# Hybrid decoder block on one core: pacing the streamed w_ada, and the order of the first projection stage

## The chip, the cores and the metric

The kernel runs on one core of a Trainium2 chip. The metric is the device time of one execution in microseconds (us). The core has a matrix engine (TensorE, in the profile PE, with its weight loads apart as PEld), VectorE (DVE), ScalarE (ACT), GpSimd (POOL) and SyncE (SP); here SP issues nearly all DMA transfers. PE accumulates in PSUM, which has eight banks.

## The reference, cut to what matters

One decoder layer for 256 tokens of width 2048, in float32. A conditioning vector c gives six modulation vectors; two projections of the normed x feed an attention and a retention branch, which are gated, merged and projected; a gated MLP with a causal convolution follows.

```python
mod = silu(c) @ w_ada + b_ada                       # 2048 x 12288
shift1, scale1, gate1, shift2, scale2, gate2 = split(mod, 6)
h = rms_norm(x, norm1_g) * (1 + scale1) + shift1
qa, ka, va, qr, kr, vr, gr, ga_logit, gb_logit = split(h @ w_in)
ya = attention(norm(qa), norm(ka), va) @ w_attn_br
yr = (group_norm(retention(rot(qr), rot(kr), vr)) * silu(gr)) @ w_ret_br
x = x + gate1 * ((sigmoid(ga_logit) * ya + sigmoid(gb_logit) * yr) @ w_o)
h2 = rms_norm(x, norm2_g) * (1 + scale2) + shift2
val, gt = split(causal_conv(h2 @ w_up))
x = x + gate2 * ((silu(gt) * val) @ w_down)
```

## The kernel before, in words

Every weight comes from memory once, in chunks of 128 partitions x 1024 columns (512 KB), through a pool of nine buffers (`raw`) that SP refills in order: a transfer is issued when the buffer of the ninth transfer before it is free. A weight chunk is split into two float32r parts, `hi` by a cast on ScalarE and `lo` by a subtraction on VectorE (`split`, lines 142 to 145; four buffers each), and PE runs three products per chunk: hi x h_h, hi x h_l, lo x h_h. The raw buffer is free when VectorE has made `lo`.

**w_ada is not multiplied on PE.** Its rows stand as 96 tiles of 128 outputs, two halves of 1024 each (`ada`, lines 192 to 201). A half is loaded into a `raw` buffer and VectorE multiplies it with silu(c) and sums along the row, in one pass. These passes are a paced generator in the class `Side` (lines 51 to 89): every weight chunk calls `side.pump()`, which adds the rate to what is due (line 82) and draws a pass for each whole unit (lines 83 to 85). `side.until` (lines 66 to 70) draws without pace until a condition holds. Three rates exist: `ADA_FIRST` for the tiles of shift1 and scale1 (64 halves), `ADA_RATE` from va on for gate1, shift2, scale2 and gate2 (128 halves, `rest_of_mod`, line 498), `ADA_LAST` behind the second norm. gate1 is asked for ahead of o_0 (line 712), and all up to scale2 ahead of o_3 (line 729): 96 of the 128.

**The first projection stage** (lines 479 to 493) makes 6144 columns for queries, keys, retention's queries and keys, and gr: six groups (g) of two blocks of 512 columns, for two halves of the tokens (t), so that a group takes four PSUM banks. The depth of 2048 is 16 tiles (k), and h's tiles appear one by one as w_ada's passes end (`modulated`, `norm_tile`). So the stage goes in three steps over k, `STEPS` (line 29): tiles 0 to 3, 4 to 9 and 10 to 15; in each step all six groups. In step 0 groups 0 and 1 share their chunks in turn, and then the others follow one by one. The first two tiles (`PLAIN`) run in plain float32 from the unsplit chunk. At a group's end `g_out` (line 469) brings the four banks into `acc`: by a copy on ScalarE in step 0, by a sum on VectorE later. `turn_x` (lines 309 to 324) scales and transposes x, a quarter of its columns at a time; quarters 0 and 1 come ahead of the stage, 2 and 3 ahead of groups 2 and 3 of step 0. At the end of a group in the last step `beside_groups` starts the side work on it (norms, turns, rotation), which also advances by `side.pump()`.

What stands between: va, attention, vr, retention, ya and ga, yr and gb; then the output projection o_0 to o_3 (line 725 on), the second norm in an order written out by hand (lines 787 to 836), and the MLP (up, dn).

The order on each engine is set by a scheduler from priorities, except for instructions marked `keep_in_program_order`, which stand in the order of the code on their engine; w_ada's passes are so marked, and chained.

Of the kernel before, what the change touches and what calls it, by code (L numbers as in the profile page):

```python
# [11 lines left out]
F32 = mybir.dt.float32  # L12
F32R = mybir.dt.float32r
AF = mybir.ActivationFunctionType
ALU = mybir.AluOpType
AX = mybir.AxisListType

P = 128
D = 2048
S = 256  # L20
KC = D // P
# [4 lines left out]
EPS = 1e-6  # L26
NG = 6
NB = 512
STEPS = ((0, 4), (4, 10), (10, 16))
PLAIN = 2  # L30
ADA_FIRST = 0.8
ADA_RATE = 0.46
ADA_LAST = 0.38
SIDE_AHEAD = 150
SKEW = 4
# [57 lines left out]
def block_kernel(ctx, tc, a, out):  # L93
    nc = tc.nc
# [9 lines left out]
    def unit(name, dt=F32, shape=(P, 2, S)):  # L104
        return upool.tile(list(shape), dt, tag="u", name=name)

    def tmp(name, shape=(P, S), dt=F32):
        return tpool.tile(list(shape), dt, tag="t", name=name)
# [4 lines left out]
    def bank(name):  # L113
        return psum.tile([P, 512], F32, tag="ps", name=name)
# [10 lines left out]
    ident = cpool.tile([P, P], F32, name="ident")  # L125
# [12 lines left out]
    def seq(ins):  # L138

        return tc.keep_in_program_order(ins) if ordered[0] else ins  # L140

    def split(hi, lo, src):

        return (seq(nc.scalar.copy(hi, src)),  # L144
                seq(nc.vector.tensor_tensor(lo, src, hi.bitcast(F32), op=ALU.subtract)))  # L145
# [39 lines left out]
    def chain(ins):  # L185

        if behind[0] is not None:
            tc.add_manual_dep(ins.ins, behind[0].ins.name, mybir.DependencyInfo(
                mybir.DependencyClass.NoSync, mybir.DependencyReason.DATA), reason="w_ada in order")
        behind[0] = ins  # L190
# [92 lines left out]
    def norm_tile(k):  # L283
        m = mod6[:, 0:2, k]
        chain(nc.vector.tensor_tensor(m, parts6[:, 0:2, k, 0], parts6[:, 0:2, k, 1], op=ALU.add))
        chain(nc.vector.tensor_tensor(m, m, bada6[:, 0:2, k], op=ALU.add))
        scale = mod6[:, 1, k:k + 1]
        chain(nc.vector.tensor_tensor(scale, scale, sm[:, C_G1 + k:C_G1 + k + 1], op=ALU.mult))
        t = plain[:, k] if k < PLAIN else tmp(f"ht_{k}")
        nc.scalar.activation(t, turned[k // 2][:, k % 2 * S:(k % 2 + 1) * S], AF.Identity,  # L290
                             bias=mod6[:, 0, k:k + 1], scale=mod6[:, 1, k:k + 1])
        h = unit(f"h1_{k}", F32R)
        split(h[:, 0], h[:, 1], t)
        return h[:, 0], h[:, 1]

    def modulated():
# [9 lines left out]
    nc.vector.tensor_reduce(rstd, ssq0.rearrange("p (t n) -> p t n", n=4), axis=AX.X, op=ALU.add)  # L306
    rstd_of(rstd, rstd, 1.0 / D)

    def turn_x(q):

        xs = []
        for t in range(2):
            xs.append(tmp(f"xn1_{q}_{t}", (P, NB)))
            ins = nc.scalar.activation(xs[t], x2[:, t, q * NB:(q + 1) * NB], AF.Copy, scale=rstd[:, t:t + 1])
            if q > 1:
                tc.keep_in_program_order(ins)
        for i in range(2):
            pt = bank(f"xn_t{q}_{i}")
            for j in range(2):
                for t in range(2):  # L320
                    s = slice((2 * i + j) * P, (2 * i + j + 1) * P)
                    nc.tensor.transpose(pt[:, (2 * j + t) * P:(2 * j + t + 1) * P], xs[t][:, s], ident)
            turned.append(unit(f"xnT_{q}_{i}", shape=(P, NB)))
            nc.scalar.copy(turned[-1], pt)

    for q in range(2):
        turn_x(q)

    acc = [[None, None] for _ in range(12)]

# [24 lines left out]
    def query_heads(n):  # L355
        for t in range(2):
            sq = tmp(f"qksq_{n}_{t}", (P, NB))
            nc.scalar.activation(sq, acc[n][t], AF.Square)
            nc.vector.tensor_reduce(ssq1[:, t, 4 * n:4 * n + 4], sq.rearrange("p (h d) -> p h d", d=P), axis=AX.X,
                                    op=ALU.add)  # L360
        yield 1
        if n < 2:
            qT[2 * n:2 * n + 2] = heads_of(n, "q")
            yield 1

    def key_scales():
        rstd_of(ssq1.rearrange("p t h -> p (t h)"), ssq1.rearrange("p t h -> p (t h)"), 1.0 / P)
        nc.vector.scalar_tensor_tensor(gg, sm[:, C_GQ:C_GQ + 1], P ** -0.5, sm[:, C_GK:C_GK + 1],
                                       op0=ALU.mult, op1=ALU.mult)
        for n in range(2, 4):  # L370
            for t in range(2):
                k = acc[n][t].rearrange("p (h d) -> p h d", d=P)
                nc.vector.tensor_tensor(k, k, ssq1[:, t, 4 * n:4 * n + 4].unsqueeze(2).to_broadcast([P, 4, P]),
                                        op=ALU.mult)
        yield 3
        for n in range(2, 4):
            kT[2 * n - 4:2 * n - 2] = heads_of(n, "k", gg)
            yield 1
# [22 lines left out]
    def bias_rows():  # L401
        psr = bank("psr")
        nc.tensor.matmul(psr[:HEADS, :383], rel, onehot, start=True, stop=True)
        brow = tmp("brow", (HEADS, 383))
        nc.vector.tensor_tensor(brow, psr[:HEADS, :383], maskrow, op=ALU.add)
        nc.sync.dma_start(bdram, brow)
        yield 1
# [14 lines left out]
    def rotated(n):  # L422
        for t in range(2):
            x = acc[n][t]
            xs = x.rearrange("p (h s d) -> p h s d", s=2, d=P // 2)
            x8 = x.rearrange("p (a d) -> p a d", d=P // 2)
            sw = tmp(f"sw_{n}_{t}", (P, 4, 2, P // 2))
            sn = sinT[:, t].rearrange("p (s d) -> p s d", s=2)
            for s in range(2):
                nc.vector.tensor_tensor(sw[:, :, s], xs[:, :, 1 - s], sn[:, s].unsqueeze(1).to_broadcast([P, 4, P // 2]),  # L430
                                        op=ALU.mult)
            nc.vector.tensor_tensor(x8, x8, cosT[:, t].unsqueeze(1).to_broadcast([P, 8, P // 2]), op=ALU.mult)
            nc.vector.tensor_tensor(x8, x8, sw.rearrange("p h s d -> p (h s) d"), op=ALU.add)
            yield 2
# [6 lines left out]
    def beside_groups(g):  # L441
        if g < 2:
            side.add(query_heads(2 * g))
            side.add(query_heads(2 * g + 1))
        elif g < 4:
            if g == 2:
                side.add(bias_rows())
                side.add(key_scales())
            side.add(rotated(2 * g))
            side.add(rotated(2 * g + 1))  # L450

    def g_chunk(banks, g, k, first, last):
        side.until(lambda: len(h1) > k)
        if k < PLAIN:
            raw = load(a["w_g"][k, g], 1024, f"g_{g}_{k}")
            for t in range(2):
                for j in range(2):
                    nc.tensor.matmul(banks[j][t], plain[:, k, t * P:(t + 1) * P], raw[:, j * NB:(j + 1) * NB],  # L458
                                     start=first, stop=last)
        else:  # L460
            hi, lo = load_split(a["w_g"][k, g], 1024, f"g_{g}_{k}")
            for part, w in ((0, hi), (1, hi), (0, lo)):
                for t in range(2):
                    for j in range(2):
                        nc.tensor.matmul(banks[j][t], tok(h1[k], part, t), w[:, j * NB:(j + 1) * NB],  # L465
                                         start=(first and part == 0 and w is hi), stop=(last and w is lo))
        side.pump()

    def g_out(step, g, banks):
        for j in range(2):  # L470
            for t in range(2):
                n = 2 * g + j
                if step == 0:
                    acc[n][t] = unit(f"acc_{n}_{t}", shape=(P, NB))
                    nc.scalar.copy(acc[n][t], banks[j][t])
                else:
                    nc.vector.tensor_tensor(acc[n][t], banks[j][t], acc[n][t], op=ALU.add)

    for step, (ka, kb) in enumerate(STEPS):
        if step == 1:  # L480
            tables()

        for gs in ((0, 1), (2,), (3,), (4,), (5,)) if step == 0 else tuple((g,) for g in range(NG)):
            if step == 0 and gs[0] in (2, 3):
                turn_x(gs[0])
            banks = {g: [[bank(f"g{step}_{g}_{j}_{t}") for t in range(2)] for j in range(2)] for g in gs}
            for k in range(ka, kb):
                for g in gs:
                    g_chunk(banks[g], g, k, k == ka, k == kb - 1)
                    if k == kb - 1:  # L490
                        g_out(step, g, banks[g])
                        if kb == KC:
                            beside_groups(g)
    side.until(lambda: len(h1) == KC)

    mods = [2 * KC]
# [21 lines left out]
    side.drain()  # L518
    side.pace(rest_of_mod(), ADA_RATE)
    for n in range(4, 8):  # L520
# [465 lines left out]
```

## Time and profile before

| | us |
|---|---|
| median of 3 runs | 1657.1 (1656.17 to 1658.59) |
| the profiled execution's own time | 1653.88 |
| its span | 1652.1 |
| PE busy | 1600.3 (97%) |
| VectorE busy | 1137.1 (69%) |
| ScalarE busy | 797.4 (48%) |

The span runs from the first to the last instruction; the execution's own time lies 1.8 us above it. Busy matmuls are modelled and overlap, so a matmul of 512 columns is listed with 0.39 us where the next one starts 0.23 us later. In a row of the timeline the time in brackets is the idle time of the engine before the row, with what ended it.

### The profile page before, as it was taken

How to read it: one execution, taken by the hardware profiler on the slowest of the kernel's cores; microseconds unless marked ns; L12 is line 12 of the kernel's file. 1: busy time of each engine (PE TensorE's matmuls, PEld its weight loads, DVE VectorE, ACT ScalarE, POOL GpSimd, SP SyncE). 2: the span in 40 equal slices, each digit the busy share in tenths (PEclk: the TensorE clock that was granted, in tenths of full speed). 3: DMA queues.
4: the chain of work that ended last, by engine and by line, in shares of the span. 5: the costliest groups of instructions: out<-in, count | busy, mean ns of one | idle time of the engine just before them, and what ended most of it. 6: DMA issues, size and time to landing. Idle time of an engine off the chain costs nothing.

```text
span 1652.1 us, 19655 instructions
## 1 busy us (share of the span) xinstructions
PE 1600.3 (97%) x7124; PEld 1303.4 (79%) x7124; DVE 1137.1 (69%) x1567; ACT 797.4 (48%) x1051; POOL 31.2 (2%) x36
## 2 busy tenths in 40 slices
PE   6899999999999999999987999999999999999998
PEld 3567778888888888888865788888888888888887
DVE  6568878877777666777768687777655566566654
ACT  4544345456545443444525665555433455555432
POOL 0000000310000000000000000000000000000000
PEclk9999999999999999999998999999999999999999
DMA  9999876677767888888868587777666666666661
GB/s 370 333 317 329 301 262 189 213 222 263 239 235 263 284 287 273 281 278 276 301 219 312 193 273 262 264 256 231 213 194 192 191 182 187 184 188 186 198 211 54
DMA packets 113194, 400.85 MB, mean 243 GB/s; under 512 B 12660, under 2 KB 15300, under 8 KB 113096
## 3 DMA queue, kind: packets, MB, share of 16 engines
q1 hardware_dynamic: 111800, 397.41, 72.2%
q10 hardware_dynamic: 1296, 2.17, 0.4%
q8 instruction: 56, 0.92, 0.2%
q14 instruction: 42, 0.34, 0.1%
HBM read 397.41 MB, written 2.13 MB: 242 GB/s over the span
## 4 chain that ended last, share of the span: by engine, by line
PE 90%; DVE 4%; DMA 3%; ACT 2%; issue 1%; SPq 0%; ACTq 0%; DVEq 0%
PE up L217 28%; PE dn L217 14%; PE g L465 10%; PE vr L217 5%; PE yr L217 5%; PE ga L217 5%; PE gb L217 5%; PE o L217 4%; PE va L217 3%; PE ya L217 3%; DVE ada L198 2%; PE g L458 2%; DMA ada<-in_w_ada 2%; DMA raw_g<-in_w_g 1%; PE ut L667 1%
## 5 line engine op out<-in xcount | busy, mean ns | idle before, releaser
L145 DVE TENSOR_TENSOR lo_up<-raw_up,hi_up 128x1024 fp32r<-128x1024 f32 x172 | 209.7, 1224 | 151.5 <-ACT hi_up L144 105.6
L217 PE MATMUL up<-hi_up,h_h 128*128 128x512 f32 x688 | 270.0, 393 | 0.0
L217 PE MATMUL up<-hi_up,h_l 128*128 128x512 f32 x688 | 268.6, 391 | 1.4 <-DVE h_l L761 1.4
L144 ACT CAST hi_up<-raw_up 128x1024 fp32r<-128x1024 f32 x172 | 181.0, 1054 | 183.6 <-PE up L217 158.8
L198 DVE SCALAR_TENSOR_TENSOR ada<-ada,crow 128x1024 f32<-128x1024 f32 x192 | 227.7, 1218 | 1.1 <-DMA ada<-in_w_ada 1.1
L217 PE MATMUL up<-lo_up,h_h 128*128 128x512 f32 x688 | 193.1, 392 | 0.0
L145 DVE TENSOR_TENSOR lo_dn<-raw_dn,hi_dn 128x1024 fp32r<-128x1024 f32 x88 | 107.8, 1225 | 107.2 <-ACT hi_dn L144 103.6
L465 PE MATMUL g<-hi_g,h 128*128 128x512 f32 x672 | 171.1, 397 | 8.9 <-ACT h L144 4.5
L465 PEld LDWEIGHTS g<-hi_g,h 128*128 128x128 f32 x672 | 127.2, 190 | 39.2 <-ACT hi_g L144 5.9
L144 ACT CAST hi_dn<-raw_dn 128x1024 fp32r<-128x1024 f32 x88 | 92.8, 1054 | 134.6 <-PE dn L217 118.7
L217 PEld LDWEIGHTS up<-hi_up,h_l 128*128 128x128 f32 x688 | 129.3, 188 | 27.9 <-DVE h_l L761 1.8
L217 PEld LDWEIGHTS up<-lo_up,h_h 128*128 128x128 f32 x688 | 129.2, 188 | 26.4
L217 PEld LDWEIGHTS up<-hi_up,h_h 128*128 128x128 f32 x688 | 129.3, 188 | 25.9 <-ACT h_h L758 0.4
L144 ACT CAST hi_g<-raw_g 128x1024 fp32r<-128x1024 f32 x84 | 88.2, 1052 | 125.5 <-DMA raw_g<-in_w_g 66.1
L217 PE MATMUL dn<-hi_dn,gT_h 128*128 128x512 f32 x352 | 137.4, 390 | 0.0
L217 PE MATMUL dn<-hi_dn,gT_l 128*128 128x512 f32 x352 | 137.1, 389 | 0.0
L145 DVE TENSOR_TENSOR lo_g<-raw_g,hi_g 128x1024 fp32r<-128x1024 f32 x84 | 101.3, 1218 | 49.1 <-ACT hi_g L144 42.2
L217 PE MATMUL dn<-lo_dn,gT_h 128*128 128x512 f32 x352 | 95.7, 390 | 0.0
L465 PE MATMUL g<-lo_g,h 128*128 128x512 f32 x336 | 91.1, 395 | 4.6 <-DVE lo_g L145 4.6
L465 PEld LDWEIGHTS g<-lo_g,h 128*128 128x128 f32 x336 | 63.2, 190 | 20.0 <-DVE lo_g L145 6.5
L217 PEld LDWEIGHTS dn<-hi_dn,gT_h 128*128 128x128 f32 x352 | 66.1, 188 | 13.7
L217 PEld LDWEIGHTS dn<-lo_dn,gT_h 128*128 128x128 f32 x352 | 66.1, 188 | 13.7
(223 smaller groups left out, 2443.1 us busy)
## 6 DMA issues: line engine op xcount, KB each, us to landing
ada<-in_w_ada SPq DMA_DIRECT2D x192, 512.0 KB, 5.2
raw_up<-in_w_up SPq DMA_DIRECT2D x172, 512.0 KB, 3.6
raw_g<-in_w_g SPq DMA_DIRECT2D x96, 512.0 KB, 5.3
raw_dn<-in_w_down SPq DMA_DIRECT2D x88, 512.0 KB, 3.7
raw_vr<-in_w_vr SPq DMA_DIRECT2D x32, 512.0 KB, 4.4
raw_ga<-in_w_col SPq DMA_DIRECT2D x32, 512.0 KB, 5.0
raw_yr<-in_w_ret_br SPq DMA_DIRECT2D x32, 512.0 KB, 4.7
raw_gb<-in_w_col SPq DMA_DIRECT2D x32, 512.0 KB, 4.5
```

Source lines behind the costliest of these rows:

```text
L144: return (seq(nc.scalar.copy(hi, src)), seq(nc.vector.tensor_tensor(lo, src, hi.bitcast(F32), op=ALU.subtract)))
L145: seq(nc.vector.tensor_tensor(lo, src, hi.bitcast(F32), op=ALU.subtract)))
L198: chain(tc.keep_in_program_order(nc.vector.scalar_tensor_tensor(t, t, 1.0, crow[:, h * 1024:(h + 1) * 1024], op0=ALU.mult, op1=ALU.mult, a ...
L217: nc.tensor.matmul(ps[t], tok(acts[k0 + k], part, t), w[:, k * NB:(k + 1) * NB], start=first, stop=last)
L458: nc.tensor.matmul(banks[j][t], plain[:, k, t * P:(t + 1) * P], raw[:, j * NB:(j + 1) * NB], start=first, stop=last)
L465: nc.tensor.matmul(banks[j][t], tok(h1[k], part, t), w[:, j * NB:(j + 1) * NB], start=(first and part == 0 and w is hi), stop=(last and w ...
L667: nc.tensor.transpose(pt[:, (2 * j + t) * P:(2 * j + t + 1) * P], us[t][:, s], ident)
```

## The change

It has four parts. `ADA_RATE` goes from 0.46 to 0.54. `STEPS` becomes tiles 0 to 2, 3 to 8 and 9 to 15. `g_out` takes the blocks to bring out; in steps 1 and 2 a group's four sums are no longer written at its end but two behind the next group's first chunk and two behind its second (`late`), and `beside_groups` follows them. `turn_x` is parted in `scale_x`, called ahead of a group, and the transposes, called behind the group's second chunk for quarters 2 and 3 and there kept in program order on PE. In `norm_tile` the cast of h's high part is kept in program order on ScalarE.

```diff
-STEPS = ((0, 4), (4, 10), (10, 16))
+STEPS = ((0, 3), (3, 9), (9, 16))
-ADA_RATE = 0.46
+ADA_RATE = 0.54
...
         h = unit(f"h1_{k}", F32R)
-        split(h[:, 0], h[:, 1], t)
+        tc.keep_in_program_order(nc.scalar.copy(h[:, 0], t))
+        nc.vector.tensor_tensor(h[:, 1], t, h[:, 0].bitcast(F32), op=ALU.subtract)
...
-    def turn_x(q):
-
+    def scale_x(q):
         xs = []
         for t in range(2):
             xs.append(tmp(f"xn1_{q}_{t}", (P, NB)))
             ins = nc.scalar.activation(xs[t], x2[:, t, q * NB:(q + 1) * NB], AF.Copy, scale=rstd[:, t:t + 1])
             if q > 1:
                 tc.keep_in_program_order(ins)
+        return xs
+
+    def turn_x(q, xs):
+
         for i in range(2):
             pt = bank(f"xn_t{q}_{i}")
             for j in range(2):
                 for t in range(2):
                     s = slice((2 * i + j) * P, (2 * i + j + 1) * P)
-                    nc.tensor.transpose(pt[:, (2 * j + t) * P:(2 * j + t + 1) * P], xs[t][:, s], ident)
+                    ins = nc.tensor.transpose(pt[:, (2 * j + t) * P:(2 * j + t + 1) * P], xs[t][:, s], ident)
+                    if q > 1:
+                        tc.keep_in_program_order(ins)
...
-    def g_out(step, g, banks):
-        for j in range(2):
+    def g_out(step, g, banks, js):
+        for j in js:
...
+    late = None
     for step, (ka, kb) in enumerate(STEPS):
...
-            if step == 0 and gs[0] in (2, 3):
-                turn_x(gs[0])
+            xs = scale_x(gs[0]) if step == 0 and gs[0] in (2, 3) else None
             banks = {g: [[bank(f"g{step}_{g}_{j}_{t}") for t in range(2)] for j in range(2)] for g in gs}
             for k in range(ka, kb):
                 for g in gs:
                     g_chunk(banks[g], g, k, k == ka, k == kb - 1)
+                    if xs and k == ka + 1:
+                        turn_x(g, xs)
+                    if late and k < ka + 2:
+
+                        g_out(*late, (k - ka,))
+                        if k == ka + 1:
+                            if late[0] == len(STEPS) - 1:
+                                beside_groups(late[1])
+                            late = None
                     if k == kb - 1:
-                        g_out(step, g, banks[g])
-                        if kb == KC:
-                            beside_groups(g)
+                        if step == 0:
+                            g_out(step, g, banks[g], range(2))
+                        else:
+                            late = (step, g, banks[g])
+    g_out(*late, range(2))
```

How this moves instructions is shown at three places, by the order in which they stand on an engine. In the names, `ada_78_0` is the first half of w_ada's tile 78, `raw_o_3_0` the chunk of tiles 0 and 1 of o_3.

**SP between o_2 and o_3.** Before; the rows ahead of these are five more of w_ada, back to `raw_o_2_14`:

```order
L196 DMA ada_76_1_6905<-in_w_ada 128x1024
L196 DMA ada_77_0_6908<-in_w_ada 128x1024
L196 DMA ada_77_1_6911<-in_w_ada 128x1024
L196 DMA ada_78_0_6914<-in_w_ada 128x1024
L196 DMA ada_78_1_6917<-in_w_ada 128x1024
L196 DMA ada_79_0_6920<-in_w_ada 128x1024
L196 DMA ada_79_1_6923<-in_w_ada 128x1024
L196 DMA ada_80_0_6929<-in_w_ada 128x1024
L173 DMA raw_o_3_0_6934<-in_w_o 128x1024
L196 DMA ada_80_1_6952<-in_w_ada 128x1024
L173 DMA raw_o_3_2_6955<-in_w_o 128x1024
```

Now:

```order
L173 DMA raw_o_2_8_6852<-in_w_o 128x1024
L173 DMA raw_o_2_10_6870<-in_w_o 128x1024
L196 DMA ada_80_1_6888<-in_w_ada 128x1024
L173 DMA raw_o_2_12_6891<-in_w_o 128x1024
L173 DMA raw_o_2_14_6909<-in_w_o 128x1024
L196 DMA ada_81_0_6927<-in_w_ada 128x1024
L173 DMA raw_o_3_0_6940<-in_w_o 128x1024
L173 DMA raw_o_3_2_6958<-in_w_o 128x1024
L196 DMA ada_81_1_6976<-in_w_ada 128x1024
```

The thirteen transfers of w_ada in a row are gone; one half stands between two or three chunks of o.

**VectorE where the second norm meets the first up block** (`h2_2_0_l` is the low half of the third quarter of h2 for the first tokens). Before:

```order
L198 SCALAR_TENSOR_TENSOR ada_81_1_7368,parts_91<-ada_81_1_7368,crow_97 128x1024
L145 TENSOR_TENSOR lo_up_0_12_7374<-raw_up_0_12_7371,hi_up_0_12_7373 128x1024
L145 TENSOR_TENSOR lo_up_0_14_7392<-raw_up_0_14_7389,hi_up_0_14_7391 128x1024
L761 TENSOR_TENSOR h2_2_0_l_7276<-ht2_2_0_7270,h2_2_0_h_7275 128x512
L743 TENSOR_SCALAR xn_3_0_7279<-x2_79,rstd2_6376 128x512
```

Now:

```order
L198 SCALAR_TENSOR_TENSOR ada_82_1_7374,parts_91<-ada_82_1_7374,crow_97 128x1024
L145 TENSOR_TENSOR lo_up_0_12_7380<-raw_up_0_12_7377,hi_up_0_12_7379 128x1024
L145 TENSOR_TENSOR lo_up_0_14_7398<-raw_up_0_14_7395,hi_up_0_14_7397 128x1024
L198 SCALAR_TENSOR_TENSOR ada_83_0_7413,parts_91<-ada_83_0_7413,crow_97 128x1024
L779 TENSOR_TENSOR h2_2_0_l_7282<-ht2_2_0_7276,h2_2_0_h_7281 128x512
L761 TENSOR_SCALAR xn_3_0_7285<-x2_79,rstd2_6415 128x512
```

One w_ada pass more stands ahead of the low half.

**PE where group 2 of step 0 begins** (`xn_t2` are the transposes of x's third quarter, `raw_g_2_0` the plain chunk of tile 0). Before:

```order
L465 MATMUL g0_1_1_1_203<-lo_g_1_3_371,h1_3_333 128x512
L322 MATMUL xn_t2_0_401<-ident_84,xn1_2_0_397 128x128
L322 MATMUL xn_t2_1_408<-ident_84,xn1_2_0_397 128x128
L458 MATMUL g0_2_0_0_415<-raw_g_2_0_419,h1_plain_138 128x512
L458 MATMUL g0_2_1_0_417<-raw_g_2_0_419,h1_plain_138 128x512
```

Now, from the second plain chunk of the group on:

```order
L464 MATMUL g0_2_0_0_342<-raw_g_2_1_355,h1_plain_138 128x512
L464 MATMUL g0_2_1_0_344<-raw_g_2_1_355,h1_plain_138 128x512
L464 MATMUL g0_2_0_1_343<-raw_g_2_1_355,h1_plain_138 128x512
L464 MATMUL g0_2_1_1_345<-raw_g_2_1_355,h1_plain_138 128x512
L326 MATMUL xn_t2_0_364<-ident_84,xn1_2_0_338 128x128
L326 MATMUL xn_t2_0_364<-ident_84,xn1_2_1_340 128x128
```

The first transposes stood ahead of the group's plain chunks, behind the last chunk of tile 3; they now stand behind both plain chunks, and tile 3 is not in this step.

## Rows read from the trace of the kernel before

**Rows 1.** Page, part 1: busy us, share, instructions.

```profile
PE 1600.3 (97%) x7124; PEld 1303.4 (79%) x7124; DVE 1137.1 (69%) x1567; ACT 797.4 (48%) x1051; POOL 31.2 (2%) x36
```

**Rows 2.** Stretches: length, busy PE PEld DVE ACT POOL (instructions), PE clock, DMA share, GB/s.

```profile
20.00:60.00 40.00, 32.87 (x95) 18.30 (x94) 28.69 (x54) 14.69 (x23) 2.51 (x3) 0.96 1.02 394
...
110.00:210.00 100.00, 91.44 (x395) 73.70 (x394) 86.14 (x135) 40.64 (x46) 0.00 (x0) 1.00 0.89 311
...
320.00:520.00 200.00, 200.00 (x954) 167.38 (x952) 149.45 (x263) 110.76 (x194) 5.66 (x10) 1.00 0.73 241
520.00:860.00 340.00, 340.00 (x1517) 281.56 (x1516) 234.91 (x274) 143.56 (x155) 2.84 (x4) 1.00 0.83 280
860.00:880.00 20.00, 5.89 (x19) 4.15 (x18) 19.93 (x34) 4.59 (x7) 3.29 (x3) 0.66 0.71 273
```

**Rows 3.** Timeline of PE, 860 to 879 us: start, length, instruction [idle before].

```profile
860.59 0.61 PE L217 MATMUL o<-lo_o,mT_h 128*128 128x512 f32 x2
875.17 0.79 PE L217 MATMUL o<-hi_o,mT_h 128*128 128x512 f32 x1 [13.96 <-ACT hi_o L144]
...
878.75 0.51 PE L217 MATMUL o<-lo_o,mT_h 128*128 128x512 f32 x1
```

**Rows 4.** Timeline of SP's issues, 836 to 869 us.

```profile
838.20 29.40 SPq L196 DMA_DIRECT2D ada<-in_w_ada  x13
868.42 0.33 SPq L173 DMA_DIRECT2D raw_o<-in_w_o  x1
```

**Rows 5.** Timeline of VectorE, 862 to 878 us.

```profile
862.58 1.22 DVE L198 SCALAR_TENSOR_TENSOR ada<-ada,crow 128x1024 f32<-128x1024 f32 x1
...
877.47 1.23 DVE L145 TENSOR_TENSOR lo_o<-raw_o,hi_o 128x1024 fp32r<-128x1024 f32 x1
```

**Rows 6.** Waits of PE, 20 to 220 us: total us, times, longest.

```profile
PE g L465 <- DVE lo_g L145: 4.6, 4, 1.9
PE g L465 <- ACT h L144: 4.5, 2, 3.1
PE g L465 <- ACT hi_g L144: 4.4, 2, 2.6
PE xn_t L322 <- ACT xn L314: 4.2, 2, 2.1
```

**Rows 7.** Chain that ended last: start, length, piece; a block of ga.

```profile
530.81 21.76 PE ga L217 x96
```

**Rows 8.** Timeline of PE, 43 to 73 us.

```profile
44.06 3.37 PE L465 MATMUL g<-hi_g,h 128*128 128x512 f32 x8 [3.06 <-ACT h L144]
...
48.80 2.00 PE L465 MATMUL g<-hi_g,h 128*128 128x512 f32 x8
...
53.78 0.44 PE L322 MATMUL xn_t<-ident,xn 128*128 128x128 f32 x2 [2.08 <-ACT xn L314]
54.06 7.03 PE L458 MATMUL g<-raw_g,h_plain 128*128 128x512 f32 x16
60.93 0.82 PE L322 MATMUL xn_t<-ident,xn 128*128 128x128 f32 x6
```

**Rows 9.** Two stretches around these waits, columns as in rows 2.

```profile
35.00:53.00 18.00, 13.34 (x48) 9.91 (x48) 14.79 (x27) 8.21 (x15) 2.51 (x3) 0.91 1.02 407
49.00:60.00 11.00, 8.92 (x28) 4.83 (x27) 4.92 (x10) 6.94 (x12) 2.04 (x2) 1.00 1.00 370
```

**Rows 10.** Timeline of VectorE: a group's four sums in step 1.

```profile
168.91 2.48 DVE L477 TENSOR_TENSOR acc<-g,acc 128x512 f32<-128x512 f32 x4
```

**Rows 11.** Timeline of VectorE: the end of the stage's last w_ada pass.

```profile
202.28 0.08 DVE L198 DVE_READ_ACCUMULATOR ada<-ada,crow 128x1 f32 x1
```

**Rows 12.** Timeline of VectorE and PE, 911 to 919 us.

```profile
912.05 2.35 DVE L145 TENSOR_TENSOR lo_up<-raw_up,hi_up 128x1024 fp32r<-128x1024 f32 x2
914.32 1.22 DVE L198 SCALAR_TENSOR_TENSOR ada<-ada,crow 128x1024 f32<-128x1024 f32 x1
...
918.48 0.50 PE L217 MATMUL up<-hi_up,h_l 128*128 128x512 f32 x1 [1.44 <-DVE h_l L761]
```

More of the change, by code (lines that the diff above doesn't have):

```diff
@@ L326, in block_kernel @@
     for q in range(2):
-        turn_x(q)
+        turn_x(q, scale_x(q))
     acc = [[None, None] for _ in range(12)]
```

## The prediction

> **What bounds the kernel now.** I read the page first: TensorE is busy 97% of the span [rows 1], so time can only come out of stretches in which it waits. The table of stretches shows where these are [rows 2]: from 320 to 860 us PE is busy all the time, and it falls short in two places: between 20 and 210 us, the first projection stage, and between 860 and 880, where it is busy 5.9 of 20 us at a granted clock of 0.66. Then I asked the timeline of PE, SyncE and VectorE what the waits are.
>
> At 860 us a flush ends the block o_2. PE's last matmul there starts at 860.59, the next at 875.17 behind an idle time of 13.96 us [rows 3]. SP issues 13 w_ada transfers in a row, with no weight of o_3 among them, and only then, at 868.42, the first chunk of o_3 [rows 4]. VectorE works off the passes one behind the other, from 862.58 to the chunk's own split at 877.47 [rows 5]: 13 passes, 1.15 us each. The code gives the reason: the line `side.until(lambda: mods[0] >= 5 * KC)` ahead of o_3 wants 96 half columns of the paced w_ada, and 184 chunks have passed by then (8 + 8 for va, 32 for vr, 16 for ya, 32 each for ga, yr and gb, 24 for o_0 to o_2). At a rate of 0.46 they have drawn 84; 12 are owed and come at once.
>
> In the first stage PE's waits are short and of four kinds [rows 6]: 17.7 us in all between 20 and 220 us. Two I can name by place [rows 8]: at 44.06 the first group's chunk of tile 3 waits 3.06 us for that tile of h, and the twelve matmuls behind it take 4.74 us (44.06 to 48.80) where a split chunk takes 12 x 0.227 = 2.72 (the pitch of 96 matmuls in 21.76 us [rows 7]), since the granted clock is down (0.91 over that stretch [rows 9]). At 53.78 x's third turn waits 2.08 us for the scaled x; x's fourth one waits as long (two waits, 4.2 us [rows 6]). The later waits are for landings: SP refills nine buffers in order, and a buffer is free only when VectorE is through with it.
>
> **The change, part by part.** The sum is made on the profiled execution, 1653.9 us, which is 3.2 below the median 1657.1 of the runs shown; at the end I add the 3.2.
>
> 1. *Rate 0.54.* 184 x 0.54 = 99.4, so 99 half columns are drawn before o_3, 3 more than wanted, and nothing is owed; the order of SP shows o_3's chunks alternating with single w_ada transfers. What goes: from the start of the last two matmuls at 860.59 to the ninth behind the wait, at 878.75, are 18.16 us in which ten matmuls run; at the pitch of 0.227 us they need 2.27. **-15.9 us.** What it costs: 15 passes of 1.15 us (17.2 us of VectorE) move into 320 to 860 us. VectorE is busy 149 of 200 and 235 of 340 us there [rows 2], so 156 us are free, and the DMA share is 0.73 and 0.83. Hidden, if single passes do not fall ahead of a split that PE waits for: from 0 (below nothing there is no way: a pass never helps PE there) up to all 17.2 us. I take 0, since the 84 passes drawn before lie in this stretch beside a PE without idle time.
>
> 2. *One pass more in the second norm.* With the paced columns three ahead, the order of VectorE has ada_83_0 between the split of up_0_14 and the low half of h2_2_0. PE waits for just that low half at 918.48, 1.44 us, with VectorE busy without a break from 912.05 [rows 12]. One pass: **+1.2 us** (the pitch 1.15). Between 0, if VectorE has a gap by then, and 1.2 I take 1.2: it has none in the rows.
>
> 3. *Steps of 3, 6 and 7 tiles, x's turns behind two chunks.* The matmuls are the same in number: 12 plain chunks of 8 x 0.43 and 84 split ones of 2.72 us. What goes at first: tile 3 is no longer wanted by the first two groups (3.06 of wait and 2.0 of slow clock), and the transposes stand behind the two plain chunks of their group, 6.87 us of work, instead of ahead of them (2 x 2.08). Together 9.3 us. What is late next: step 1 begins after 18 chunks and not after 24, so PE has 6 x 2.72 = 16.3 us less work in hand when it asks for tiles 5 to 8 and for w_g of the next group. The transfers ahead fall as well: in SP's order the last w_ada transfer of the stage stands behind 57 chunks of w_g instead of 58, 121 against 122 with its 64 own. In the run before, that last pass ends at 202.28 [rows 11]. So at the same rate of the ring the stage is one transfer earlier, at 311 GB/s [rows 2] 0.524 MB / 311 = 1.7 us; with all that PE saves early handed on it is 9.3; if all named waits went, 17.7 and 2.0 of slow clock. On the other side, if tiles 6 and 7 or 8 are each waited for as tile 3 is now, 2 x 3.06 = +6.1. Between -19.7 and +6.1 I take **-1.7**: the last waits of the stage are the ring's, and the row of the ring is the nearest.
>
> 4. *Group sums two at a time behind the next group's first chunks.* Four sums take 2.48 us on VectorE [rows 10]; their number stays. The wait that is added is one for banks: two groups use all eight, and a group's four are free only when its sums are done, now up to two chunks later. They are wanted again a group later (six or seven chunks, 16 to 19 us), so I cost it at 0; without that cover the price is one set of sums per change of group (rival D). Queued behind a late sum on VectorE are the splits of the next chunks.
>
> 5. *The rest:* the scaling of x goes to ScalarE a group's chunks earlier, h's copies there stay in program order, the tables' three transfers and POOL's markers come with the earlier first sum, and the side work begins two chunks later with 12 chunks left, as before. All of it lies beside PE's matmuls (ScalarE is busy 40.6 of the 100 us from 110 to 210 [rows 2]): 0.
>
> Sum: -15.9 + 1.2 - 1.7 = -16.4; 1637.5 on the profiled scale, **1640.7 us** against the median.
>
> One bound can be held against a page. The transfers of the first stage ran at 394 GB/s between 20 and 60 us and at 311 from 110 to 210 [rows 2]: by the first rate the 100 us could shrink to 79, so the 17.7 us of waits may all go. The Trainium skill ("DMA: Bandwidth & Descriptors", Specifications) puts the HBM side of one core at about 358 GB/s, by which they could shrink to 87 only, and some 13 us of the waits at most would go. The trace speaks against that limit, since 394 was measured over 40 us.
>
> **The rivals.**
>
> *B: the first stage keeps what it saves early.* The 9.3 us of item 3 stay, since PE is also on the chain there and frees buffers earlier. For: the plain chunks' buffers are freed by PE itself. Against: the waits at the end of the stage are landings, and the transfers ahead of them are as many. -15.9 + 1.2 - 9.3 = -24.0: 1633, at the utmost 1623 (-34.4).
>
> *C: the first stage loses.* Tiles 6 to 8 come late twice: -15.9 + 1.2 + 6.1 = -8.6: 1648.5.
>
> *D, slower: the late sums hold the banks.* At each of the 11 changes of group in steps 1 and 2 PE waits for one set of sums, 2.48 us: 27.3 in all, and -14.7 + 27.3 = +12.6: 1670. It decides from 1.34 us per change on (14.7 / 11). For: q's turns take four banks between groups 1 and 2 of the last step, so there the next group does need the late ones. Against: no change of group shows a wait for VectorE's sums in the rows of PE's waits [rows 6]. Short waits need not slow the clock here: behind the 2.08 us at 53.78 it was granted in full (49 to 60 us, 1.00 [rows 9]). The Trainium skill ("TensorE: Matmul & The Clock Gate", A second HAM failure mode: psum-queue depth-cycling) says that a PE which idles briefly at each turn of the banks has its clock cut again and again; by that rule each change would also cost the 2.0 us seen behind tile 3, 22 more, and D would stand at 1692. The row at 53.78 is against it.
>
> *E: nothing is won.* The passes of the flush come back as waits in va to o, where attention and retention already share VectorE: -15.9 + 17.2 + 1.2 - 1.7 = +0.8: 1658. For: VectorE's passes are strictly in order, so each one ahead of a split delays it. Against: 156 us are free.
>
> **How the numbers follow.** My forecast 0.55, B 0.20, C 0.15, D 0.05, E 0.05. A measurement can tell about 0.2% (3.3 us) from no change. The forecast, B and C are faster by more: 0.90; E is the same: 0.05; D is slower: 0.05. The range reaches from 1630 (most of B) to 1649 (C); D, E and the far half of B are left out, under 2 in 10.
>
> **What would show it.** Right: PE without idle time from 855 to 890, w_ada passes single between o's splits; no wait of 3 us near 44 and none for the scaled x; last w_ada pass of the first stage at 198 to 203 us; the wait for h2_2_0's low half 2.6 us instead of 1.44. Wrong: a gap of PE over 2 us around o_3, PE idle between 320 and 860, waits on VectorE's sums at changes of group, or a last w_ada pass under 195 or over 207.

## The result, and the profile of the changed kernel

The changed kernel takes 1636.73 us (median of four runs, 1633.6 to 1637.11); the kernel before, run beside it, 1656.63 (1654.8 to 1658.59). The ratio is 0.9876, 95% interval [0.9858, 0.9893]: 19.9 us faster. The forecast was 1640.7, its range 1630 to 1649. The profiled execution took 1636.67 us, its span is 1634.9. The four runs had mean granted clocks of TensorE of 0.994 to 0.999, and the one at 0.999 is the shortest, 1633.6.

Page, part 1, of the changed kernel, beside [rows 1]. What went is idle time of PE: span less busy time was 1652.1 - 1600.3 = 51.8 us and is 1634.9 - 1603.5 = 31.4.

```profile
PE 1603.5 (98%) x7124; PEld 1305.9 (80%) x7124; DVE 1135.5 (69%) x1567; ACT 799.0 (49%) x1051; POOL 28.8 (2%) x36
```

The table of stretches of the changed kernel, columns as in [rows 2]:

```profile
20.00:60.00 40.00, 39.62 (x119) 21.21 (x118) 26.47 (x52) 17.50 (x31) 2.27 (x3) 1.00 1.02 393
60.00:110.00 50.00, 43.99 (x153) 30.44 (x152) 34.48 (x59) 22.41 (x34) 0.00 (x0) 0.93 0.91 335
110.00:210.00 100.00, 95.34 (x403) 77.18 (x402) 85.06 (x131) 40.84 (x47) 0.00 (x0) 0.97 0.88 303
...
880.00:924.00 44.00, 39.88 (x176) 31.00 (x175) 26.62 (x37) 30.63 (x59) 0.00 (x0) 0.96 0.53 169
```

Three things are to be seen. From 20 to 60 us PE is now busy 39.62 of 40, where it was busy 32.87 [rows 2]: the early waits are gone. From 60 to 110 it is busy only 43.99 of 50 and the granted clock is 0.93. And 110 to 210 gains 4 us of busy time, at a clock of 0.97 instead of 1.00. From 320 to 860 PE is busy without a break, as before.

The waits of PE between 20 and 220 us, columns as in [rows 6]:

```profile
PE g L471 <- ACT h L293: 6.0, 2, 4.7
PE g L471 <- DVE lo_g L145: 4.7, 3, 2.5
```

The scaled x is waited for no more. The longest wait is now for h, and it lies in the first group of step 1, at its tiles 6 and 7 (timeline of PE, 89 to 100 us):

```profile
90.56 2.11 PE L471 MATMUL g<-hi_g,h 128*128 128x512 f32 x8 [1.32 <-ACT h L293]
...
98.27 2.07 PE L471 MATMUL g<-hi_g,h 128*128 128x512 f32 x4 [4.69 <-ACT h L293]
```

At o_3 the flush of [rows 3] to [rows 5] is gone: on VectorE the passes come one at a time among the last splits of o_3 (timeline of VectorE, 856 to 868 us), and PE runs without a wait from 320 us to the second norm at 878.

```profile
855.70 1.22 DVE L198 SCALAR_TENSOR_TENSOR ada<-ada,crow 128x1024 f32<-128x1024 f32 x1
...
858.05 1.22 DVE L145 TENSOR_TENSOR lo_o<-raw_o,hi_o 128x1024 fp32r<-128x1024 f32 x1
...
862.79 1.22 DVE L145 TENSOR_TENSOR lo_o<-raw_o,hi_o 128x1024 fp32r<-128x1024 f32 x1
863.92 1.22 DVE L198 SCALAR_TENSOR_TENSOR ada<-ada,crow 128x1024 f32<-128x1024 f32 x1
```

The second norm is where the change loses. VectorE and PE there, to be held against [rows 12]:

```profile
894.84 1.22 DVE L198 SCALAR_TENSOR_TENSOR ada<-ada,crow 128x1024 f32<-128x1024 f32 x1
...
895.99 2.35 DVE L145 TENSOR_TENSOR lo_up<-raw_up,hi_up 128x1024 fp32r<-128x1024 f32 x2
898.26 1.22 DVE L198 SCALAR_TENSOR_TENSOR ada<-ada,crow 128x1024 f32<-128x1024 f32 x1
...
899.40 0.69 DVE L779 TENSOR_TENSOR h_l<-ht,h_h 128x512 fp32r<-128x512 f32 x1
```

```profile
897.04 0.50 PE L217 MATMUL up<-hi_up,h_h 128*128 128x512 f32 x1
899.10 0.49 PE L217 MATMUL up<-hi_up,h_h 128*128 128x512 f32 x1 [1.56 <-ACT h_h L776]
900.14 0.79 PE L217 MATMUL up<-hi_up,h_l 128*128 128x512 f32 x1 [0.55 <-DVE h_l L779]
900.74 0.63 PE L217 MATMUL up<-hi_up,h_h 128*128 128x512 f32 x1
901.16 0.63 PE L217 MATMUL up<-hi_up,h_l 128*128 128x512 f32 x1
```

The second pass stands ahead of the low half as the order showed. PE now takes the high half for the other tokens first, which ScalarE makes, and the low half behind it, so the one wait of 1.44 has become two, of 1.56 and 0.55. Behind the two waits the matmuls come 0.42 apart instead of 0.23, until 903.24: the granted clock is at its lower level of 1.2 GHz, which it was not behind the single wait of 1.44 [rows 12].

The time by stage, read from the first matmul of each block on PE's timeline (us):

| stage | before | changed | difference | forecast |
|---|---|---|---|---|
| first g to first va | 300.65 | 297.37 | -3.3 | -1.7 |
| va to o_0 | 474.94 | 474.99 | 0 | 0 |
| o_0 to the first up | 106.48 | 90.44 | -16.0 | -15.9 |
| first up to first dn | 256.47 | 258.74 | +2.3 | +1.2 |

This adds to 17.0; the profiled executions are 17.2 apart (1653.88 to 1636.67), the medians 19.9. The experiments take up where the other 2.7 come from.

### The profile page after: what moved, and what is told of

Read it like the earlier page. It is cut to its first block, busy times and chain, and to the rows that moved or that the text cites. A ratio compares the mean times of both kernels' runs of the same rounds, so it can differ in the third digit from the quotient of the medians.

```text
span 1634.9 us, 19648 instructions
## 1 busy us (share of the span) xinstructions
PE 1603.5 (98%) x7124; PEld 1305.9 (80%) x7124; DVE 1135.5 (69%) x1567; ACT 799.0 (49%) x1051; POOL 28.8 (2%) x36
## 5 line engine op out<-in xcount | busy, mean ns | idle before, releaser
L217 PE MATMUL up<-lo_up,h_h 128*128 128x512 f32 x688 | 193.4, 393 | 0.0
L471 PE MATMUL g<-lo_g,h 128*128 128x512 f32 x336 | 94.4, 400 | 4.7 <-DVE lo_g L145 4.7
L217 PEld LDWEIGHTS dn<-lo_dn,gT_h 128*128 128x128 f32 x352 | 66.1, 188 | 13.7
L217 PEld LDWEIGHTS dn<-hi_dn,gT_l 128*128 128x128 f32 x352 | 66.1, 188 | 13.6
```

Of the source, the lines that this page charges most:

```text
L217: nc.tensor.matmul(ps[t], tok(acts[k0 + k], part, t), w[:, k * NB:(k + 1) * NB], start=first, stop=last)
```

## The experiments

Four questions: is the flush's price one per owed pass, what does a pass at the second norm cost, which part of the first stage's change does what, and why do medians and profiles differ. Times are medians in us; the kernel before had medians of 1656.6 to 1657.3 beside them. The stages are read as in the table above.

### The two halves alone

`rate_only`:

```diff
 # the kernel before
-ADA_RATE = 0.46
+ADA_RATE = 0.54
```

> The kernel before with ADA_RATE 0.54 and nothing else of the change. Theory, the rate alone ends the row of owed passes ahead of o_3 and brings a second pass into the second norm: from va on the kernel should lie as the changed one, -16.0 at o's block and +2.3 at the second norm, so 13.7 us below before, about 1643 on the scale on which before has 1656.6; the first stage keeps its early waits of 3.06 and 2.08. Rival, the two halves of the change need each other (the first stage's new order is what makes room for the 15 passes between va and o): less than 10 us are gained.

1639.85; ratio 0.9896 [0.9881, 0.991], 17.4 us below before. By stages: o_0 to up 90.44, exactly the changed kernel's; up to dn 257.34, +0.9; the first stage, which this edit does not touch, 302.64 where the profile of before has 300.65. The 13.7 forecast were too few: the second pass at the norm cost 1.4 less here than in the changed kernel, and the rest is within what the first stage differs by from one execution to the next (`before_again` below). The rival (under 10) is out.

`stage_only`:

```diff
 # the changed kernel
-ADA_RATE = 0.54
+ADA_RATE = 0.46
```

> The changed kernel with ADA_RATE back at 0.46: only the first stage's parts are left. Theory: 3.5 us below before (va's first matmul 3.5 us earlier), about 1653, with PE's wait of about 16 us ahead of o_3 back and the second norm as before (one pass ahead of the low half, a wait of 1.44). Rival, the 3.5 us are an accident of one profile: within 1 us of before.

1650.85; ratio 0.996 [0.9946, 0.9974], 6.4 below before, where 3.5 were expected; PE waits 14.15 us ahead of o_3 again, and the norm is as before (256.40).

So the flush is the rate's alone, and the first stage's part is worth more by medians (6.4) than by the two profiles (3.3). `before_again`, the kernel before once more and unchanged, was run for this difference.

> The kernel before, unchanged, once more with a profile. Theory, its profiled run (1653.88) was at the low end of what the first stage's waits allow, since the slow clock behind them differs from run to run: a new profile lies above 1655 with more slow clock between 20 and 110 us. Rival, the profile costs nothing but reads low by 3 us always: it lies 3 us below its median again.

1657.4 (median of 10), ratio 1.0005 [0.9995, 1.0014]. Its profiled execution took 1657.65 us, span 1655.9. The stretches, against 0.96 and 32.87 for the first one in [rows 2]:

```profile
20.00:60.00 40.00, 34.64 (x94) 19.81 (x93) 28.56 (x54) 14.68 (x23) 2.21 (x3) 0.91 1.00 388
60.00:110.00 50.00, 47.92 (x165) 29.99 (x163) 26.97 (x45) 22.06 (x34) 0.00 (x0) 0.97 0.87 307
```

The waits for tile 3 and for x are the same (3.06, 2.08, 2.08), and one for a chunk's high part at 35 us is even shorter (0.22 instead of 1.80); but the lower clock lasts longer, and the first stage takes 304.20 us instead of 300.65. The granted clock is 0.83 from 36 to 56 us (0.91 in the first profile), 0.88 from 64 to 78 (1.00), and 0.77 from 205 to 220 (0.89), so not only the early waits have it behind them. The later stages agree within 0.4. One program's first stage thus differs by 3.5 us between two executions, with the clock that is granted. The prediction was made on one of the quicker ones, and no run here shows what decides between them. Against `before_again` the changed kernel's stage gains 6.8, close to the 6.4 that `stage_only` shows by medians.

### How the price of owed passes runs

`owed_8` and `owed_5`:

```diff
 # the changed kernel
-ADA_RATE = 0.54
+ADA_RATE = 0.48      # owed_8
+ADA_RATE = 0.50      # owed_5
```

> The changed kernel with ADA_RATE 0.48: 184 x 0.48 = 88 halves drawn where 96 are asked for, about 8 owed ahead of o_3, and one pass at the second norm as before. Theory A, VectorE: the owed passes that the nine buffers force ahead of o_3's first low part stand behind o_2's sum on VectorE, 9 of them here at 1.147 us, so PE waits 10 to 12 us ahead of o_3; the second norm gives back 2.3; about 1645. Theory B, transfers: each owed half costs its own transfer, 1.32 us, 8 x 1.32 = 10.6, less 2.3, also about 1645. Both the same here; the next kernel parts them.

1647.52; ratio 0.994 [0.9926, 0.9955]. o_0 to up takes 103.40: 13.0 more than with nothing owed, of which 7.41 and 1.78 are waits and the rest is a clock of 0.66 between 860 and 880.

> The changed kernel with ADA_RATE 0.50: 92 halves drawn, six in a row ahead of o_3's first chunk on the queue (five owed). Theory A, VectorE: six owed halves and o_3's first chunks fit in the nine buffers together, so on VectorE the passes may stand behind o_3's low parts, and PE does not wait for them: 0 to 1 us at o_3; with only one pass at the second norm 2.3 us come back, so about 1635, below the changed kernel. Theory B, transfers: 5 x 1.32 = 6.6 us of wait ahead of o_3, less 2.3, about 1641.

1635.31; ratio 0.987 [0.9855, 0.9884]. o_0 to up 91.89: only 1.45 more than with nothing owed. VectorE in `owed_8`, where nine passes stand behind o_2's sum and ahead of o_3's low parts:

```profile
857.08 0.69 DVE L739 TENSOR_TENSOR og<-o,gate 128x512 f32<-128x512 f32 x1 [6.93 <-PE o L217]
...
859.78 1.22 DVE L198 SCALAR_TENSOR_TENSOR ada<-ada,crow 128x1024 f32<-128x1024 f32 x1
...
870.09 2.38 DVE L145 TENSOR_TENSOR lo_o<-raw_o,hi_o 128x1024 fp32r<-128x1024 f32 x2
```

and in `owed_5`, where the low part of o_3 comes first and seven passes behind it:

```profile
857.38 1.23 DVE L145 TENSOR_TENSOR lo_o<-raw_o,hi_o 128x1024 fp32r<-128x1024 f32 x1
...
859.12 1.22 DVE L198 SCALAR_TENSOR_TENSOR ada<-ada,crow 128x1024 f32<-128x1024 f32 x1
...
867.17 4.91 DVE L145 TENSOR_TENSOR ho_l<-raw_ho,ho_h 128x512 fp32r<-128x512 f32 x8
```

The first row of `owed_8` is the reason: VectorE idles 6.93 us for PE to end o_2, because the sum of o_2 stands ahead of the passes in its order, and all the owed halves sit in their buffers meanwhile. As long as the six transfers in a row leave room in the nine buffers for o_3's first chunks, these are split ahead of the passes, and PE has work. Ten in a row, as in `owed_8`, leave none. So theory A holds: 0, 5, 8 and 12 owed cost 0, 1.45, 13.0 and 16.0 to 16.9 us at o. At 1.32 each, 5 would have cost 6.6. Where between 5 and 8 the price jumps was not measured. The 1.45 of `owed_5` are low parts made while PE uses them: two matmuls of ho_4 then start every 0.60 us instead of every 0.45 (867.92, 868.52, 869.12 on PE's timeline), eight times.

### The passes at the second norm

`norm_clear`:

```diff
 # the changed kernel
-    side.rate = ADA_LAST
+    side.rate, side.due = ADA_LAST, -1.0
```

> The changed kernel (rate 0.54) with what is due of w_ada set to -1 behind the second norm, so that neither of its two passes stands on VectorE ahead of h2_2_0's low half; they are made later. Theory: the passes are what up's first half waits for: up's first matmul to dn's first was 258.74 in the changed kernel against 256.47 before with one pass; with none at least the 2.3 come back and up to 1 us more, 1633 to 1634.5 against 1636.7. Rival, ScalarE's high half of the other token half (899.05 in the changed kernel) binds whatever VectorE does: less than 1 us.

1632.66; ratio 0.9851 [0.9836, 0.9865], 4.1 below the changed kernel. PE at the place, with both passes gone from VectorE:

```profile
895.68 0.50 PE L217 MATMUL up<-hi_up,h_h 128*128 128x512 f32 x1
896.49 0.50 PE L217 MATMUL up<-hi_up,h_l 128*128 128x512 f32 x1 [0.31 <-DVE h_l L779]
896.82 0.39 PE L217 MATMUL up<-hi_up,h_h 128*128 128x512 f32 x1
```

First up to first dn is 255.35 here (255.33 in `both_edits`), 256.40 to 256.50 in the five profiles with one pass, 257.34 in `rate_only` with two passes at full clock, and 258.7 to 260.2 in the six with two passes and a lower one. A pass costs about 1.0, and the lower clock behind two passes 1.4 or more. ScalarE's high half does not bind: without the passes the order of PE has the low half next, and it waits 0.31 for it.

### The first stage, part by part

`turns_ahead`, `sums_at_end`, `steps_4_6_6` and `first_090` are one edit each of the changed kernel; `steps_3_5_8` is one edit of `first_090`:

```diff
 # turns_ahead
-            xs = scale_x(gs[0]) if step == 0 and gs[0] in (2, 3) else None
+            if step == 0 and gs[0] in (2, 3):
+                turn_x(gs[0], scale_x(gs[0]))
...
-                    if xs and k == ka + 1:
-                        turn_x(g, xs)
 # sums_at_end
-                        if step == 0:
-                            g_out(step, g, banks[g], range(2))
-                        else:
-                            late = (step, g, banks[g])
-    g_out(*late, range(2))
+                        g_out(step, g, banks[g], range(2))
+                        if kb == KC:
+                            beside_groups(g)
 # steps_4_6_6
-STEPS = ((0, 3), (3, 9), (9, 16))
+STEPS = ((0, 4), (4, 10), (10, 16))
 # first_090; steps_3_5_8 has this line too
-ADA_FIRST = 0.8
+ADA_FIRST = 0.9
 # steps_3_5_8
-STEPS = ((0, 3), (3, 9), (9, 16))
+STEPS = ((0, 3), (3, 8), (8, 16))
```

> The changed kernel with x's transposes back ahead of groups 2 and 3, all else as changed. Theory of the prediction's item 3, PE's early waits are tied to what comes later by the ring: two waits of about 2.1 us for scaled x come back (and perhaps a slow clock of 2 us behind them), but the waits of 6.0 for h at 90 to 98 shrink by as much, since h's tiles come when memory brings them: 0 to 2, 1636.7 to 1639. Rival, the turns are worth their waits in full: +4.2 to +6, 1641 to 1643.

1643.78; ratio 0.9923 [0.99, 0.9946], 7.1 above the changed kernel. The waits for scaled x come back in full (2.08 and 2.07), and those at tiles 6 and 7 in step 1 do not shrink. They are 3.17 for h and 5.05 for the high part of a chunk of w_g (timeline of PE), 8.2 in all where the changed kernel has 6.0:

```profile
99.63 3.78 PE L471 MATMUL g<-hi_g,h 128*128 128x512 f32 x8 [3.17 <-ACT h L293]
...
110.17 5.48 PE L471 MATMUL g<-hi_g,h 128*128 128x512 f32 x12 [5.05 <-ACT hi_g L144]
```

The clock from 60 to 110 us is 0.92, and memory moves 271 GB/s there instead of 335. The early waits are not made up for later, as the theory had it. Why memory moves less was not looked into.

> The changed kernel with each group's four sums at the group's end again, the rest as changed. Theory of the prediction's item 4, the place of the sums is worth nothing: 1636.7, 1.5 either way. Rival, four sums in a row (2.48 us) make the next group's low parts late, as the waits for low parts of 1.4 to 2.6 in the kernel before: +2 to +6, 1639 to 1643.

1636.41; ratio 0.9883 [0.9869, 0.9898]: the same as the changed kernel. With steps of 3, 6 and 7 the place of the sums is worth nothing.

> The changed kernel with the steps of before (tiles 0 to 3, 4 to 9, 10 to 15); x's turns, late sums and the rate as changed. Theory, the waits of the first stage are a balance of memory against PE: tile 3 is late again by 3 us near 44, but step 1 begins some 16 us later with four halves more to bring (5.2 us), so the 6.0 us of waits near 90 to 98 go: -3 to 0, 1633.5 to 1637. Rival, three tiles first is worth its own wait of 3 us and what follows: +2 to +4, 1639 to 1641.

1625.71; ratio 0.9819 [0.9803, 0.9836]. This is the fastest kernel of the study, 11.0 below the changed one and 31 below before, and faster than theory and rival allowed. Its stretches and its waits of PE between 20 and 220 us:

```profile
20.00:60.00 40.00, 36.78 (x111) 21.26 (x110) 30.17 (x57) 15.98 (x26) 2.64 (x3) 0.96 1.03 401
60.00:110.00 50.00, 50.00 (x183) 33.45 (x182) 31.93 (x54) 23.79 (x37) 0.00 (x0) 1.00 0.91 335
110.00:210.00 100.00, 98.09 (x430) 80.20 (x429) 91.30 (x144) 45.34 (x51) 0.00 (x0) 1.00 0.94 336
```

```profile
PE g L471 <- ACT h L293: 3.0, 1, 3.0
PE g L471 <- ACT hi_g L144: 1.2, 2, 1.0
...
PE g L471 <- DVE lo_g L145: 0.8, 1, 0.8
```

The one wait for tile 3 is back (3.01 at 43.91) with the lower clock behind it. Step 1 begins at 102.0 us instead of 80.9, and PE is busy all of 60 to 110, with 183 matmuls where the changed kernel has 153, and 430 instead of 403 from 110 to 210. Memory moves 335 GB/s in the first of these two stretches in both kernels, but 336 instead of 303 in the second. That a PE that waits frees its buffers late, and so slows the ring, fits these rows; no run sets this apart from the work in hand.

What the first stage loses can be added up from two things, PE's waits and the time lost to the lower clock (one less the granted clock, times the stretch):

| | waits | lower clock | stage | rest |
|---|---|---|---|---|
| before | 17.6 | 3.4 | 300.65 | 279.7 |
| `before_again` | 16.0 | 8.5 | 304.20 | 279.7 |
| changed | 11.0 | 6.8 | 297.37 | 279.5 |
| `turns_ahead` | 16.6 | 8.5 | 304.87 | 279.7 |
| `steps_4_6_6` | 5.1 | 1.7 | 286.39 | 279.6 |

The rest, PE's own work, is the same in these five (277.3 to 281.5 over all fourteen profiles). So of the 11 us between the changed kernel and `steps_4_6_6`, 6 are waits and 5 are clock.

> The changed kernel with ADA_FIRST 0.9. Theory, the waits for h at 90 to 98 us are the memory's: the transfers that stand ahead of tile 8's last half on the queue are the same in number, only in another order, so the 6 us stay within 1.5 and the time within 2 of 1636.7. Rival, the waits are the pacing's: tiles 6 to 8 come earlier, up to 6 us and the slow clock behind them go, 1630.

1632.34; ratio 0.9848 [0.9833, 0.9863], 4.4 below the changed kernel: more than the theory allowed and less than the rival. One of the two waits for h goes and the other is 3.69 instead of 4.69; the last tile's last pass starts at 193.4 instead of 214.7. The pacing thus binds in part. SP's queue in the changed kernel shows where (timeline of SP, 50 to 112 us):

```profile
76.54 8.21 SPq L196 DMA_DIRECT2D ada<-in_w_ada  x4
85.56 0.33 SPq L173 DMA_DIRECT2D raw_g<-in_w_g  x1
86.71 5.75 SPq L196 DMA_DIRECT2D ada<-in_w_ada  x4
```

The first group of step 1 asks for a new tile of h with every chunk, four halves of w_ada each, and the pace of 0.8 has not drawn them. `side.until` in `g_chunk` then draws them at once: a small flush of the kind that stood ahead of o_3. `steps_4_6_6` has such rows too (four halves from 97.63 on), with 24 chunks of PE's work ahead of them instead of 18.

> Steps of 3, 5 and 8 tiles with ADA_FIRST 0.9, the rest as changed: step 1's first group needs tile 7 last, not tile 8, and four halves fewer stand ahead of its last chunk. Theory, memory-bound up to there: 4 x 1.31 = 5.2 us earlier, the wait of 4.69 near 98 goes; the group of step 2 that needs all 16 tiles comes four chunks of groups earlier and may wait up to 3; net -2 to -6, 1631 to 1635. Rival, the four transfers come back as waits for low parts in step 2's first group: 0, 1637.

1641.92; ratio 0.9906 [0.9891, 0.992], 9.6 above `first_090`: both theories missed, since it is slower. The wait for h near 95 shrinks to 0.88, as expected, but four others take its place: 3.50 at 118.65, 2.16, 3.58 and 4.50 at 199.70, for parts of w_g. The last two fall in step 2's first group, where the rival put them. Step 1 begins with as much work done as in `first_090`; step 2 begins after 48 chunks instead of 54, at 172.8 us instead of 193.5. A step begun with less work done is slower here too.

The first stage (first g to first va) over all profiles:

| steps | x's turns | sums | us |
|---|---|---|---|
| 4, 6, 6 | ahead | at the end | 300.65, 304.20, 302.64 |
| 4, 6, 6 | behind two chunks | late | 286.39 |
| 3, 6, 7 | ahead | late | 304.87 |
| 3, 6, 7 | behind two chunks | at the end | 297.86 |
| 3, 6, 7 | behind two chunks | late | 296.24 to 298.56 (five) |
| 3, 6, 7, ADA_FIRST 0.9 | behind two chunks | late | 293.61, 293.37 |
| 3, 5, 8, ADA_FIRST 0.9 | behind two chunks | late | 302.32 |

### A faster version

`both_edits` is the changed kernel with ADA_FIRST at 0.9 and the edit of `norm_clear`.

> The changed kernel with ADA_FIRST 0.9 and, behind the second norm, what is due of w_ada set to -1. Theory, the two lie in different stages and add: 1632.3 - 4.1 = 1628.3, within 1.5. Rival, the pass that moves out of the first stage or out of the norm comes back elsewhere: above 1631.

1629.36; ratio 0.9839 [0.9825, 0.9854]: the two add within 1.1. `steps_4_6_6`, with one edit, is faster still. It still has both passes at the second norm (258.86), so the edit of `norm_clear` should be worth some 3.5 more on it (258.86 less 255.35); that was not run.

## Why the prediction was right, and where it was not

**The flush (item 1): right, in size and in reason.** -15.9 forecast, -16.0 measured by the blocks' first matmuls, and `rate_only` has the same 90.44 us from o_0 to up. The 15 passes moved to earlier blocks cost nothing: va to o_0 takes 474.99 after 474.94. Rival E is out. The sign of PE without idle time from 855 to 890 holds up to 878 us; behind that stand the second norm's own waits of 0.30 to 0.87, as in the kernel before. What the prediction did not see is that the price has a step in it: five owed passes would have cost 1.45.

**The second norm (item 2): right in kind, too small.** +1.2 forecast, +2.3 measured. The pass itself costs about 1.0; the term left out the lower clock behind the waits, 1.4. Under rival D the prediction had argued from [rows 9] that short waits need not slow the clock, which did not hold here. Nor does it hold for the wait of 2.08 that was its case: in `rate_only`, whose first stage is the same program, the granted clock is below 1 behind both waits for scaled x (0.76 from 53 to 60 us and from 70 to 77), and in `before_again` behind the second (0.76 from 70 to 77). The wait was forecast as 2.6 for the low half; it came as two, 2.1 in all.

**The first stage (item 3): the direction right, the term wrong.** -1.7 forecast; -3.3 against the profile in hand, -6.4 by medians. Two steps failed. The first is that steps and turns were costed as one edit with one sum: at the turns' new place the steps of 3, 6 and 7 cost 11 us (286.39 to 297.37), while turns, late sums and the order of h's casts together gain 14 to 18 at the old steps (300.65 to 304.20, to 286.39). The rows had both sides: the 4.2 us for scaled x and their clock, and the 16.3 us less work in hand when step 1 asks for tiles 5 to 8. The prediction named that second price as late next, bounded it at +6.1, and then took the ring's landings for what binds. The waits of 6.0 at 90 and 98 us with the low clock of 0.93 are the larger part of that price, and the waits for low parts behind 150 us with theirs the rest. That it is the work in hand that makes the difference is argued from where the waits lie; no run changed it alone. The second is the row: 202.28 of [rows 11] ends the last pass of tile 14, not of the stage. The stage's last pass, of tile 15, starts at 221.47 before and at 214.73 now (timelines of VectorE, 205 to 240 us):

```profile
221.47 1.22 DVE L198 SCALAR_TENSOR_TENSOR ada<-ada,crow 128x1024 f32<-128x1024 f32 x1
```

```profile
214.73 1.22 DVE L198 SCALAR_TENSOR_TENSOR ada<-ada,crow 128x1024 f32<-128x1024 f32 x1
```

The sign read from the row (198 to 203 right, over 207 wrong) therefore said nothing. The pass comes 6.7 us earlier, where one transfer, 1.7, was forecast.

**Late sums (item 4): 0, right.** `sums_at_end` shows it at these steps, and no wait of PE is for a sum. Rival D is out, so the rule of the Trainium skill weighed beside it ("TensorE: Matmul & The Clock Gate", A second HAM failure mode: psum-queue depth-cycling) was not tested: no run here has a wait for a bank at a change of group. Whether late sums help at steps of 4, 6 and 6, where VectorE is busy 91 of 100 us from 110 to 210, was not tried, nor the order of h's casts alone.

**Rivals B and C.** B, that the first stage keeps 9.3, lies nearer to the 6.4 of the medians than the forecast of 1.7 does, for another reason than B gave: not all that is won early is kept, but more is won (14 to 18) and 11 is paid back. C's late tiles came too: 6.0 of waits, with 6.1 forecast.

**The 3.2 us added for the median.** They are no constant that carries over from one kernel to the next. The profile of before was one of its quicker executions, by the clock that it was granted; the changed kernel's profile (1636.67) lies at its median (1636.73). The changed kernel, which waits nowhere over 0.4 us from 20 to 90 us in its profile, spreads as far (3.5 us) as the kernel before (3.8). This step put most of the 4 us on the forecast: without it the sum says 1637.5, 0.8 from the profile. That this is so near is partly luck, since the misses of items 2 and 3 (+1.1 and -1.6) nearly cancel; against the medians the change of 16.4 is 3.5 too small.

The bound of 358 GB/s that the prediction held against its rows fares no better in the later runs: between 20 and 60 us the changed kernel moves 393 GB/s and every profile here 388 to 403, over the 358 of the Trainium skill ("DMA: Bandwidth & Descriptors", Specifications).

## What to carry to other kernels

Owed work that is flushed at a deadline was nearly free here as long as the ring held it together with the next block's first chunks, and cost its whole length and the lower clock behind it once it did not, so look at what stands ahead of it on the engine's own order. Cost edits that pull against each other one by one: here one part of a winning change cost 11 us, and taking it out was the best edit of all. Take the profile of a kernel with waits twice before you trust it within 3 us.

## What the runs showed of the hardware that was not expected

The same two waits of PE, 1.55 and 0.55 us with one matmul between them, were followed by the full clock in one profile (`rate_only`, granted clock 1.00 from 880 to 924 us) and by the lower one in the six others that have them (0.92 to 0.96), among them the changed kernel with 1.56 and 0.55. In `rate_only` the matmuls behind them come 0.23 apart:

```profile
903.87 0.49 PE L217 MATMUL up<-hi_up,h_h 128*128 128x512 f32 x1 [1.55 <-ACT h_h L758]
904.92 0.50 PE L217 MATMUL up<-hi_up,h_l 128*128 128x512 f32 x1 [0.56 <-DVE h_l L761]
905.26 0.40 PE L217 MATMUL up<-hi_up,h_h 128*128 128x512 f32 x1
905.49 0.40 PE L217 MATMUL up<-hi_up,h_l 128*128 128x512 f32 x1
```

A single wait of 1.44 to 1.47 at this place, in five profiles, was never followed by the lower clock. And the kernel before, unchanged, had a granted clock of 0.96 and of 0.91 from 20 to 60 us in two executions; the one with the lower clock had the shorter waits (0.22 instead of 1.80 at 35 us, the others there alike).
